# Where four weight sets of an FFN lie in their buffers: 0, 16, 32 and 48 bytes in, not 64

## The chip, the cores and the metric

The kernel runs on one core of one Trainium2 chip. The metric is the device time of one execution in microseconds (us), lower is better; the time before is the median of three runs.

## The reference

One layer of a streaming encoder over 512 positions and 1,024 channels, all in float32: an RMS norm, one wide input projection, three mixers (pooling, a gated linear recurrence, stick-breaking attention), a gated sum of their projections, an output projection with residual, and behind that an FFN. The change lies in the FFN, which is

```python
h2 = rms_norm(x, norm_ffn[l])
act = jax.nn.silu(jnp.einsum('bsd,df->bsf', h2, w_ffn_gate[l])) * jnp.einsum('bsd,df->bsf', h2, w_ffn_up[l])
x = x + jnp.einsum('bsf,fd->bsd', act, w_ffn_down[l])
```

with 2,816 inner columns, and `rms_norm` divides by the root of the mean square over the channels.

## The kernel before

**Products.** TensorE is fed with numbers of reduced width (`F32R`). To keep the accuracy, each operand is split into a high part and a low part (ScalarE copies the high part, VectorE subtracts it from the operand), and each product takes three matmuls: high by high, high by low, low by high. Large products are computed as 2 by 2 blocks with seven block products in place of eight (Strassen's scheme in Winograd's form). The seven are called "11", "12", "S1", "S2", "S3", "S4" and "22". Where this is done, half of the 512 positions go through a matmul at a time, so a matmul there has 256 columns; elsewhere it has 512.

**A weight set.** One of the seven block products of one chunk needs one weight set: 128 partitions by 1,024 elements, as a high and a low tile. It feeds 24 matmuls: 2 column groups, 4 steps along the contraction, 3 matmuls each. Each set is loaded (a `raw`, `wr`, `wa`, `wb` or `wc` tile), perhaps summed with another block, and split into two tiles of the pools `whi` and `wlo`. Each of these pools has three buffers, so a split waits until TensorE is done with the set three places earlier.

**Offsets.** A buffer of these pools has 1,024 + 128 elements, and the set can lie anywhere in the first part of it: `weight_tiles` takes the offset `o` in elements of 4 bytes. Three constants and lists matter: `OFF = 16` (64 bytes) is the usual offset of a set in the seven-product stages; `STEPS = (0, 4, 8, 12)` (0, 16, 32 and 48 bytes) is used up by the first four sets of each such stage; sets of the other stages lie at 0. There are four stages with sets of this kind: the gates (`goffs`), the third branch projection (`boffs`), the FFN's gate and up projection, and the down projection (both `offs`).

In the program's layout a buffer of `whi` or `wlo` starts 96 bytes behind a multiple of 128, and so does each operand tile that streams through the weights in these stages. A set at 64 bytes therefore starts 32 bytes behind a multiple of 128.

**The FFN's loop.** `steps` lists 77 weight sets: pairs of chunks of 256 inner columns, for each pair the seven products in `ORDER7`, each product for both chunks of the pair, and at the end one chunk alone. In the loop over `steps` the sets are split three ahead by `make_a(n + 3)`; `made[0]` counts the sets that were split. `split_a` takes the next offset from `offs`, or `OFF` when it is empty. `product7` issues the 24 matmuls (the line recorded as L1466), L1333 and L1336 are the splits.

**The mean square.** The FFN's norm is applied late: the products run on the unnormalised input, and the factor `rb2` is multiplied into the results. The sum of squares over the channels is a matmul with a matrix of ones, `rms2` (L1436): four matmuls of 256 columns, all with the same weights `onesr`. It is called in front of step 12 (counted from 0), so it stands in TensorE's queue between the sets 12 and 13. Sets 13 and 14 are "S4" of the chunks 0 and 1, sets 15 and 16 "11" of the chunks 2 and 3. `onesr` is a slice that begins `OFF` elements into its own tile; as laid out, this slice starts 96 bytes behind a multiple of 128.

Of the kernel before, what the change touches and what calls it, by code (L numbers as in the profile page):

```python
# [65 lines left out]
def layer_kernel(ctx: ExitStack, tc: tile.TileContext, x, xt, vecs, w_in, w_qkv7, w_gate7, w_pool, w_rg, w_ig,  # L66
# [1186 lines left out]
    with ExitStack() as ffn:  # L1253
# [21 lines left out]
        A = {}  # L1275
        made = [0, 0, 0]
        offs = []

        def fsrc(c, nm):
            return w_ff7[c, CH[nm], KH[nm]]  # L1280
# [8 lines left out]
        def load_to(upto):  # L1289
            while made[1] < min(upto, DOWN):  # L1290
                load_a(made[1])
                made[1] += 1

        def fetch_a(upto):
            while made[2] < min(upto, len(steps)):
                c, nm = steps[made[2]]
                made[2] += 1
                if nm in ("12", "22"):
                    WR[c, nm] = t = wp.tile([P, 2, 4, P], F32, tag="raw", name=f"wr{c}_{nm}")
                    nc.sync.dma_start(t, fsrc(c, nm))  # L1300

        def sum_a(c):
            if c < DOWN and c not in WC:
                WC[c] = (g4 if c < 2 else corner)([2, 4, P], f"wc{c}")
                i = dve.tensor_tensor(WC[c], WB[c], WA[c], ALU.add)
                if c >= 2:
                    tc.keep_in_program_order(i)

        def make_a(upto):
            while made[0] < min(upto, len(steps)):  # L1310
                c, nm = steps[made[0]]
                made[0] += 1
                if made[0] == 1:
                    offs.extend(STEPS)
                load_to(steps[min(made[0] + 11, len(steps) - 1)][0] + 1)
                fetch_a(made[0])
                src = WR.pop((c, nm)) if nm in ("12", "22") else {"1": WB, "2": WC, "4": WC}.get(nm[1:], WA)[c] \
                    if nm[0] == "S" else WA[c]
                A[c, nm] = split_a(src, f"f{c}_{nm}", 5 < made[0] < 10)
                if nm == "11":  # L1320
                    sum_a(c)
                    nc.gpsimd.dma_start(WA[c], fsrc(c, "21"), accum_op=ALU.add)
                if nm == "S2" and c < LAST:
                    nc.gpsimd.dma_start(WC[c], fsrc(c, "12"), accum_op=ALU.add)
                if nm == "12" and c == LAST:
                    dve.tensor_tensor(WC[c], WC[c], src, ALU.add)
                fetch_a(made[0] + 2)

        def split_a(src, n, pin=False):
            o = offs.pop(0) if offs else OFF  # L1330
            h, l = (t.rearrange("p (w k c) -> p w k c", w=2, k=4)
                    for t in weight_tiles("wh" + n, "wl" + n, o))
            i = act(h, src, AF.Copy)  # L1333
            if pin:
                tc.keep_in_program_order(i)
            dve.tensor_tensor(l, src, h.bitcast(F32), ALU.subtract)  # L1336
            return h, l
# [23 lines left out]
        def in_place_t(nm, half):  # L1361
            hold["t", nm] = t = hold["t", "S1"]
            for c in range(2):
                v = t[:, 2 * c:2 * c + 2, :]
                dve.scalar_tensor_tensor(v, v, -1.0, ys[2 + c][:, :, half], ALU.mult, ALU.subtract)
            split_b(nm)
# [7 lines left out]
        for c in range(4):  # L1374
# [10 lines left out]
            if c == 3:  # L1385
                make_a(3)
# [86 lines left out]
        def split_act(kc):  # L1473
            if kc < NF // 2:
# [7 lines left out]
                 "22": ("y", 0, True, None, None), "S4": ("x", 1, False, None, None)}  # L1482
        banks, parts = {}, {}
        after = {2: [lambda: in_place_t("S2", hi)], 5: [third_t], 7: [lambda: in_place_t("22", lo)], 9: [rms2_sum],
                 12: [rms2]}
        for n, (c, nm) in enumerate(steps):
            for f in after.get(n, ()):
                f()
            if (c, nm) == (LAST, "12"):
                split_act(KD)  # L1490
            make_a(n + 3)
            z, half, first_, t_, ts_ = PLAN7[nm]
            if (c, z) not in banks:
                banks[c, z] = fp.tile([P, 2, S], F32, tag="mm", name=f"ps_{z}{c}")
            ps = banks[c, z]
            product7(A.pop((c, nm)), BF[nm], ps, half, first_)
            if t_ is not None:
                if (c, t_) not in parts:
                    parts[c, t_] = g4([2, S], f"t{t_}{c}")
                with tc.high_priority(EARLY):  # L1500
                    act(parts[c, t_][:, :, ts_], ps[:, :, hi], AF.Copy, scale=-1.0 if t_ == "y" else 1.0)
            if bg and n >= 18:
                bg.pop(0)()
            tx, ty = parts[c, "x"], parts.get((c, "y"))
            if nm == "22":
                dve.tensor_tensor(ty, ty, ps, ALU.subtract)
            if nm == "S4":
                dve.tensor_tensor(tx, tx, ps, ALU.add)
            if nm == (LONE if c == LAST else ORDER7)[-1]:
                acts.append(tx)  # L1510
                bg.extend([lambda t=ty: scaled(t), lambda t=tx: scaled(t), lambda x=tx, y=ty: gated_act(x, y)])
            if nm == "S3" and c < LAST:
                sum_a(min(c + 2, LAST))
# [211 lines left out]
```

## Time and profile before

| what | us |
|---|---|
| median of 3 runs | 903.66 (903.24 to 904.38) |
| the profiled execution, whole time | 903.32 |
| the profiled execution, span of the instructions | 901.5 |
| TensorE, matmuls busy | 895.3 |
| VectorE busy | 723.3 |
| ScalarE busy | 531.2 |

PE stands for TensorE's matmuls, PEld for its weight loads, DVE for VectorE, ACT for ScalarE, POOL for GpSimd, SP for SyncE. The matmuls of a stream overlap (one of 256 columns is recorded with some 280 ns), so what one costs in the stream is the distance from its start to the next one's, not its own duration. The chain of waits is the work that ended last, followed back from the end; a row of it gives the start, the length and the number of instructions that follow each other on one line, and its length by that number is the pace.

### The profile page before, as it was taken

How to read it: one execution, taken by the hardware profiler on the slowest of the kernel's cores; microseconds unless marked ns; L12 is line 12 of the kernel's file. 1: busy time of each engine (PE TensorE's matmuls, PEld its weight loads, DVE VectorE, ACT ScalarE, POOL GpSimd, SP SyncE). 2: the span in 40 equal slices, each digit the busy share in tenths (PEclk: the TensorE clock that was granted, in tenths of full speed). 3: DMA queues.
4: the chain of work that ended last, by engine and by line, in shares of the span. 5: the costliest groups of instructions: out<-in, count | busy, mean ns of one | idle time of the engine just before them, and what ended most of it. 6: DMA issues, size and time to landing. Idle time of an engine off the chain costs nothing.

```text
span 901.5 us, 14312 instructions
## 1 busy us (share of the span) xinstructions
PE 895.3 (99%) x5641; PEld 803.8 (89%) x5641; DVE 723.3 (80%) x900; ACT 531.2 (59%) x737; POOL 114.3 (13%) x158
## 2 busy tenths in 40 slices
PE   8999999999999999999999999999999999999998
PEld 6888778888899888888888988999999999989998
DVE  6797887988786599967887694999769596988884
ACT  7554989556856556555664544676555554653542
POOL 2010002232323101000001100111111110101200
PEclk9999999999999999999999999999999999999999
DMA  9495336798682786644635967979677776846842
GB/s 342 130 305 158 117 117 214 219 298 251 179 264 71 232 235 192 217 118 144 214 98 148 196 184 245 260 184 198 157 184 202 172 171 203 202 150 126 196 100 94
DMA packets 85283, 168.77 MB, mean 187 GB/s; under 512 B 8032, under 2 KB 48992, under 8 KB 85216
## 3 DMA queue, kind: packets, MB, share of 16 engines
q1 hardware_dynamic: 68368, 107.24, 35.6%
q0 software_dynamic: 16560, 60.30, 31.0%
q8 instruction: 44, 0.72, 0.3%
q10 hardware_dynamic: 288, 0.32, 0.1%
q14 instruction: 23, 0.19, 0.1%
HBM read 147.39 MB, written 18.87 MB: 184 GB/s over the span
## 4 chain that ended last, share of the span: by engine, by line
PE 94%; DVE 2%; ACT 2%; issue 1%; DMA 0%; ACTq 0%; DVEq 0%
PE ps_y L1466 14%; PE ps_x L1466 10%; PE ps_q L795 7%; PE ps_dy L283 5%; PE ps_dx L283 4%; PE ps_br L274 3%; PE ps_br L275 3%; PE ps_br L276 3%; PE ps_bY L1235 2%; PE ps_gate L698 2%; PE ps_gy L283 2%; PE ps_gate L276 2%; PE ps_bX L1235 2%; PE ps_gx L283 2%; PE ps_gate L275 2%; PE ps_gate L274 2%
## 5 line engine op out<-in xcount | busy, mean ns | idle before, releaser
L109 ACT ACTIVATE whi<-raw 128x1024 fp32r<-128x1024 f32 x65 | 68.8, 1058 | 79.2 <-PE ps_br L275 14.7
L110 DVE TENSOR_TENSOR wlo<-raw,whi 128x1024 fp32r<-128x1024 f32 x65 | 79.3, 1219 | 36.1 <-ACT whi L109 35.9
L110 DVE TENSOR_TENSOR wlo<-qw,whi 128x1024 fp32r<-128x1024 f32 x48 | 58.5, 1221 | 20.8 <-ACT whi L109 20.5
L109 ACT ACTIVATE whi<-qw 128x1024 fp32r<-128x1024 f32 x48 | 50.7, 1057 | 33.1 <-PE ps_q L795 18.6
L1333 ACT ACTIVATE whf_S<-wc 128x1024 fp32r<-128x1024 f32 x22 | 23.3, 1060 | 23.3 <-PE ps_y L1466 12.6
L1336 DVE TENSOR_TENSOR wlf_S<-wc,whf_S 128x1024 fp32r<-128x1024 f32 x22 | 26.9, 1221 | 12.4 <-ACT whf_S L1333 12.3
L1336 DVE TENSOR_TENSOR wlf<-wr,whf 128x1024 fp32r<-128x1024 f32 x22 | 26.8, 1220 | 8.5 <-ACT whf L1333 8.4
L1333 ACT ACTIVATE whf<-wr 128x1024 fp32r<-128x1024 f32 x22 | 23.3, 1060 | 14.9 <-PE ps_y L1466 11.9
L1051 DVE TENSOR_TENSOR_SCAN E<-K,ahead 128x512 f32<-128x512 f32 (+3 forms) x32 | 25.3, 812 | 4.4 <-ACT K L1047 4.4
L1333 ACT ACTIVATE whdS<-dw 128x1024 fp32r<-128x1024 f32 x16 | 17.0, 1064 | 19.1 <-PE ps_dy L283 9.9
L274 PE MATMUL ps_br<-yHH,whi 128*128 128x512 f32 x64 | 25.3, 395 | 0.0
L274 PE MATMUL ps_lru<-HH,whi 128*128 128x512 f32 x64 | 25.2, 394 | 0.0
L274 PE MATMUL ps_br<-yph,whi 128*128 128x512 f32 x64 | 25.2, 394 | 0.0
L274 PE MATMUL ps_pool<-HH,whi 128*128 128x512 f32 x64 | 25.2, 394 | 0.0
L274 PE MATMUL ps_gate<-HH,whi 128*128 128x512 f32 x64 | 25.0, 391 | 0.0
L275 PE MATMUL ps_br<-ypl,whi 128*128 128x512 f32 x64 | 25.0, 391 | 0.0
L276 PE MATMUL ps_br<-yph,wlo 128*128 128x512 f32 x64 | 25.0, 391 | 0.0
L276 PE MATMUL ps_gate<-HH,wlo 128*128 128x512 f32 x64 | 25.0, 391 | 0.0
L275 PE MATMUL ps_br<-yHL,whi 128*128 128x512 f32 x64 | 25.0, 390 | 0.0
L276 PE MATMUL ps_pool<-HH,wlo 128*128 128x512 f32 x64 | 25.0, 390 | 0.0
L276 PE MATMUL ps_br<-yHH,wlo 128*128 128x512 f32 x64 | 25.0, 390 | 0.0
L275 PE MATMUL ps_pool<-HL,whi 128*128 128x512 f32 x64 | 25.0, 390 | 0.0
(706 smaller groups left out, 3558.0 us busy)
## 6 DMA issues: line engine op xcount, KB each, us to landing
raw<-in_w_in_dram SPq DMA_DIRECT2D x31, 512.0 KB, 5.3
qw<-in_w_qkv_dram SPq DMA_DIRECT2D x24, 512.0 KB, 6.7
wr<-in_w_ff_dram SPq DMA_DIRECT2D x22, 512.0 KB, 3.9
raw<-in_w_branch_dram SPq DMA_DIRECT2D x16, 512.0 KB, 3.8
dw<-in_w_down_dram POOLq DMA_DIRECT2D x16, 512.0 KB, 6.3
qw<-in_w_qkv_dram POOLq DMA_DIRECT2D x12, 512.0 KB, 7.9
qd<-r POOLq DMA_DIRECT2D x12, 512.0 KB, 7.3
at<-qd SPq DMA_DIRECT2D x24, 256.0 KB, 5.6
```

Source lines behind the costliest of these rows:

```text
L109: act(hi, raw, AF.Copy)
L110: dve.tensor_tensor(lo, raw, hi.bitcast(F32), ALU.subtract)
L274: nc.tensor.matmul(ps, lh, rh, start=start, stop=False, skip_group_check=skip)
L275: nc.tensor.matmul(ps, lh, rl, start=False, stop=False, skip_group_check=skip)
L276: nc.tensor.matmul(ps, ll, rh, start=False, stop=stop, skip_group_check=skip)
L283: nc.tensor.matmul(o, a_[a][:, w, k, :], b_[b][:, k, :], start=first and n == k == 0, stop=last and n == 2 and k == 3, skip_group_check=True)
L795: nc.tensor.matmul(ps[:, a, :], b_[:, k, ts_], a_[:, kk, :], start=first and n == k == 0, stop=n == 2 and k == 3, skip_group_check=True)
L1051: dve.tensor_tensor_scan(E[:, c0:c0 + n][:, ::-1], K[:, c0 + 1:c0 + n + 1][:, ::-1], ahead[:, S - n:][:, ::-1], 0.0, ALU.mult, ALU.add)
L1235: nc.tensor.matmul(o, ah[x_][:, w, k, :], b[k][y_], start=first_ and n == k == 0, stop=n == 2 and k == 3, skip_group_check=True)
L1333: i = act(h, src, AF.Copy)
L1336: dve.tensor_tensor(l, src, h.bitcast(F32), ALU.subtract)
L1466: m = nc.tensor.matmul(o, a_[x_][:, w, k, :], b_[k][y_], start=first and n == k == 0, stop=n == 2 and k == 3, skip_group_check=True)
```

## The change

The list `STEPS` is put into `offs` a second time, in front of the set with which `made[0]` reaches 13, so that sets 13 to 16 lie 0, 16, 32 and 48 bytes into their buffers; from set 17 on it is 64 again. The step at which `rms2` is called gets a name and stays 12. In the built program no instruction is added, taken away or moved on any of the five queues; the start addresses of the weights of 96 matmuls, and of the 8 splits that write them, are all that differs.

```diff
+        RMS_AT = 12
...
             while made[0] < min(upto, len(steps)):
                 c, nm = steps[made[0]]
                 made[0] += 1
-                if made[0] == 1:
+                if made[0] in (1, RMS_AT + 1):
                     offs.extend(STEPS)
...
         after = {2: [lambda: in_place_t("S2", hi)], 5: [third_t], 7: [lambda: in_place_t("22", lo)], 9: [rms2_sum],
-                 12: [rms2]}
+                 RMS_AT: [rms2]}
```

## The prediction

> **What bounds the kernel now.** I read the page first (busy times, then the chain), then the chain of waits in order of time for the stages whose matmuls are 256 columns wide, and last the single instructions at the seams that it shows.
>
> ```profile
> PE 895.3 (99%) x5641; PEld 803.8 (89%) x5641; DVE 723.3 (80%) x900; ACT 531.2 (59%) x737; POOL 114.3 (13%) x158
> PE 94%; DVE 2%; ACT 2%; issue 1%; DMA 0%; ACTq 0%; DVEq 0%
> PE ps_y L1466 14%; PE ps_x L1466 10%; PE ps_q L795 7%; PE ps_dy L283 5%; PE ps_dx L283 4%; PE ps_br L274 3%; PE ps_br L275 3%; PE ps_br L276 3%; PE ps_bY L1235 2%; PE ps_gate L698 2%; PE ps_gy L283 2%; PE ps_gate L276 2%; PE ps_bX L1235 2%; PE ps_gx L283 2%; PE ps_gate L275 2%; PE ps_gate L274 2%
> ```
>
> TensorE is the bound: the chain that ends last lies on it for 94% of the span, and the FFN's seven-product loop (L1466) alone is 14 + 10 = 24%. So what counts is how fast TensorE takes its matmuls one after the other. A weight set is 24 matmuls of 256 columns. Here is that loop in the chain of waits (start us, us, what, number of matmuls), with rows left out where the same lengths repeat:
>
> ```profile
> 571.43 5.71 PE ps_y L1466 x48
> 577.14 11.11 PE ps_x L1466 x96
> 588.25 16.32 PE ps_y L1466 x144
> 604.57 0.48 PE ps_rms L1436 x4
> 605.04 5.65 PE ps_x L1466 x48
> 610.70 5.65 PE ps_y L1466 x48
> 616.35 11.31 PE ps_x L1466 x96
> 627.66 16.96 PE ps_y L1466 x144
> ...
> 746.38 16.96 PE ps_y L1466 x144
> ```
>
> The same instruction at the same shape has two paces. Sets 7 to 12 take 16.32 us for 144 matmuls: 113.3 ns each, 2.72 us a set. Then come the four matmuls of the mean square, and from there on the same 144 take 16.96 us: 117.8 ns each, 2.827 us a set, unchanged from 605 to the loop's end. Nothing waits at that seam, and the granted clock (the column of 1.00) is full on both sides of it:
>
> ```profile
> core 0: us, PE busy (x) PEld busy (x) DVE busy (x) ACT busy (x) POOL busy (x), PEclk, DMA share, GB/s
> 588.00:604.00 16.00, 16.00 (x144) 16.00 (x143) 14.66 (x14) 11.76 (x15) 1.69 (x2) 1.00 0.83 201
> 605.00:625.00 20.00, 20.00 (x172) 20.00 (x171) 19.77 (x22) 13.74 (x19) 2.53 (x3) 1.00 0.81 176
> 705.00:745.00 40.00, 40.00 (x342) 40.00 (x341) 30.87 (x29) 21.05 (x26) 4.22 (x5) 1.00 0.69 173
> ```
>
> So the slow pace is neither the clock nor a late operand: it is a state of TensorE's own stream, and it lasts once entered. The other three stages with 256-wide matmuls show how it is left. Gates, branch, and down projection, from the same view:
>
> ```profile
> 260.99 2.87 PE ps_gy L283 x24
> 263.86 2.84 PE ps_gx L283 x24
> 266.71 2.84 PE ps_gy L283 x24
> 269.55 2.83 PE ps_gx L283 x24
> 272.37 2.72 PE ps_gy L283 x24
> ...
> 489.03 2.87 PE ps_bY L1235 x24
> 491.90 5.68 PE ps_bX L1235 x48
> 497.58 2.83 PE ps_bY L1235 x24
> 500.41 2.72 PE ps_bX L1235 x24
> ...
> 821.45 11.38 PE ps_dy L283 x96
> 832.83 21.76 PE ps_dx L283 x192
> ```
>
> In each, four sets run at 2.87, 2.84, 2.84 and 2.83 us, and from the fifth on every set takes 2.72. Those four are the sets which lie 0, 16, 32 and 48 bytes into their buffers, and the fifth is the first at 64. The FFN does it too (5.71 for sets 1 and 2; 11.11 less two sets of 2.72 leaves 5.67 for 3 and 4). Four of four climbs end in the fast pace.
>
> **The change, part by part.** The program's instructions, their order on each queue and their number stay as they are; only the start addresses of 96 matmuls' weights (and of the splits by ScalarE and VectorE that write them) move, in sets 13 to 16.
>
> *Sets 13 to 16.* Now they take 5.65 + 5.65 = 11.30 us. If they repeat the climb, they take what the down projection's row shows for its four: 11.38. Cost: 0.08 us, all on the path.
>
> *Sets 17 to 77.* These are 61 sets at 64 bytes, now at 16.96/6 = 2.827 us. At the fast pace each takes 16.32/6 = 2.72. Gain: 61 x 0.1067 = 6.51 us, all on the path.
>
> *Why I take the fast pace.* What must be like the four known cases is the state from which the climb starts. The first set of a stage, at 0 bytes, falls into a beat of 120 ns; the mean square's matmuls do the same before set 13 begins. Weight loads of set 1, and then of the seam:
>
> ```profile
> 571.50 0.19 PEld L1466 LDWEIGHTS ps_y<-h2h,whf 128*128 128x128 f32 x1
> 571.62 0.19 PEld L1466 LDWEIGHTS ps_y<-h2l,whf 128*128 128x128 f32 x1
> 571.74 0.19 PEld L1466 LDWEIGHTS ps_y<-h2h,wlf 128*128 128x128 f32 x1
> ...
> 604.29 0.54 PEld L1436 LDWEIGHTS ps_rms<-sqr,onesr 128*128 128x128 f32 x4
> 604.76 0.19 PEld L1466 LDWEIGHTS ps_x<-h2h,whf_S 128*128 128x128 f32 x1
> ```
>
> In set 1 the loads start 0.12 us apart. At the seam, four loads of the ones fill 604.29 to 604.76, some 118 ns each, and their matmuls 604.57 to 605.04 (0.48 us, 120 ns each). The addresses agree: as the program lays them out, the slice of ones starts 96 bytes behind a multiple of 128, as a set at 0 bytes does, while a set at 64 bytes starts 32 behind one. So today the stream goes from the ones straight to sets at 64 bytes, the jump that no stage start makes, and stays slow. After the change set 13 has the phase of the ones, and the rest is the climb of the other stages. One difference remains: they come from 512-wide matmuls, this one from four 256-wide ones. For the fast pace without it there is only the price of today, 2.827; with it, 2.72. I take 2.72, by four rows against one difference.
>
> *Splits.* ACT and DVE write the same 1,024 elements to other addresses; sets 1 to 4 already have these offsets. Taken as 0; were a split 0.1 us longer, it would vanish in the slack below.
>
> *What hides behind the faster pace.* TensorE must find its weights ready. The splits wait for TensorE to give buffers back (three per kind), not for loads:
>
> ```profile
> ACT whf_S L1333 <- PE ps_x L1466: 24.8, 17, 1.8
> ACT whf_S L1333 <- PE ps_y L1466: 19.7, 14, 1.8
> ACT whf L1333 <- PE ps_y L1466: 19.3, 17, 1.8
> ```
>
> (who waited for whom between 560 and 790; us, times, longest). No split in that list waits for a DMA. Splits tied to the release move along with TensorE. The one tight place is set 19, where VectorE, busy 19.77 of 20 us with the inverse root and the first scalings, is late:
>
> ```profile
> 620.15 2.35 DVE L1336 TENSOR_TENSOR wlf<-wr,whf 128x1024 fp32r<-128x1024 f32 x2
> ...
> 621.96 0.19 PEld L1466 LDWEIGHTS ps_x<-h2h,wlf 128*128 128x128 f32 x1
> ```
>
> The first of those two subtractions (620.15 and half of 2.35: about 621.4) is needed at 621.96: 0.6 us to spare. After the change TensorE is there 0.08 later for the climb and 2 x 0.107 earlier for sets 17 and 18: 621.83, about 0.45 to spare. VectorE's work before it hangs on sets 13 and 14, which move by under 0.1. Without that cover, the cost is the missing tenths of a microsecond, and a possible fall out of the fast pace (a rival). Beyond 625, VectorE is busy 30.87 of 40; the same work in 38.5 us is 80%, which still fits.
>
> *Behind the loop.* The down projection starts some 6.4 us earlier with its loads tied to the same buffers; its 512-wide matmuls and its own climb are not touched. Taken as 0.
>
> *Sum.* +0.08 - 6.51 = -6.43 us. The profiled execution took 903.32 us (901.5 of span and 1.8 around it), which gives 896.9; the median of the three runs is 903.66, 0.34 above, so I say **897.2**.
>
> **Rivals.**
>
> *No effect: the climb doesn't work from here.* The address of a weight would matter nothing, or the four cases turned fast through what went before (512-wide matmuls), not through the offsets. Sets 17 to 77 stay at 2.827 and sets 13 to 16 cost 0 to 0.08: 903.7. For it speaks that the start differs, and that in the branch stage one set at 64 bytes right behind 512-wide matmuls and a wait came out at nearly the fast pace without any climb:
>
> ```profile
> 526.48 0.23 PE ps_out L275
> 526.71 2.76 PE ps_bY L1235 x24
> ```
>
> So the climb isn't the only way in. Against it: the four climbs switch at the same set, though what ran before differs (gates behind query products, FFN behind the output projection). The Trainium skill, "TensorE: Matmul & The Clock Gate", in the steps of "What happens when you issue a matmul", says that TensorE has two independent read ports into SBUF, so that loading the next weights takes nothing from the running matmul; by that, the weights' address would cost nothing and the time would stay at 903.7. The trace doesn't agree that nothing else sets the pace: 120, 117.8 and 113.3 ns stand for one shape at one clock. Chance 0.09.
>
> *Slower: the climb ends in the worse beat.* The offsets move the stream out of today's 117.8 ns and leave it at the 120 ns of set 1 (2.87 to 2.88 us a set). The price is 61 x (2.88 - 2.827) = 3.2 us, with 0.1 for the climb: 907.0. It decides at set 17: its loads would start 0.12 apart. For it: 120 ns is a beat that holds for a whole set; against it: in no row does a set at 64 bytes keep it. Chance 0.03.
>
> *Fast, then lost.* The climb works, TensorE waits for set 19, and falls back to 117.8 ns. Then the gain is 2 x 0.107 less 0.08: 903.5. For it: the thin 0.45 us; against it: the wait at 526 above ended in the fast pace, not out of it. Were it lost somewhere else, evenly over the loop, half the gain is left: 900.4. Chance 0.04 for both.
>
> **How the numbers follow.** The climb works: 0.84, and the time is 897.2. The measured medians of a kernel differ by some tenths (903.24 to 904.38 in three runs), so its own range is 896.2 to 898.4. That is more than 0.8 already, so the range needn't reach to the rivals at 903.5 and above; for a stall of a tenth at set 19 I put 0.1 at either end: 896.1 to 898.5. 0.2% is 1.8 us, about what a measurement of this kernel can tell from no change. Faster: 0.84 and the half of the lost cases that are lost midway, 0.86; same: no effect and the other half, 0.11; slower: 0.03.
>
> **What would show it.** In the chain of waits after 604.57, two rows of 48 that add up to about 11.38; then rows of 96 at 10.88 and of 144 at 16.32 in place of 11.31 and 16.96, up to a loop end at about 782.3 in place of 788.8. Weight loads of set 17 would start 0.113 apart. Down projection: again 11.38, then 21.76 for 192. No idle time of TensorE at 621.8. The forecast is wrong if set 17 keeps 2.83 (no effect) or 2.88 (slower), or if rows of 144 turn from 16.32 to 16.96 midway (lost).

## The result and the profile after

The changed kernel takes 897.05 us (median of 4 runs, 896.80 to 898.33) against 903.79 for the kernel before (4 runs): a ratio of 0.9928, 95% interval 0.9911 to 0.9945. The profiled execution took 896.80 us, of which 895.0 are its span. In the chain of waits (start us, us, what, number of matmuls; the code stands one line lower, so the loop is L1467 now):

```profile
571.14 5.71 PE ps_y L1467 x48
576.85 11.16 PE ps_x L1467 x96
588.01 16.45 PE ps_y L1467 x144
604.46 0.48 PE ps_rms L1437 x4
604.94 5.72 PE ps_x L1467 x48
610.66 5.67 PE ps_y L1467 x48
616.33 10.88 PE ps_x L1467 x96
627.21 16.32 PE ps_y L1467 x144
...
741.45 16.32 PE ps_y L1467 x144
...
814.91 11.38 PE ps_dy L283 x96
826.29 21.76 PE ps_dx L283 x192
```

Up to the mean square the loop is as before, but for two short waits (11.16 in place of 11.11, 16.45 in place of 16.32). Sets 13 to 16 take 5.72 + 5.67 = 11.39 us. From set 17 on, 96 matmuls take 10.88 and 144 take 16.32, up to the loop's end at 782.25 (779.53 and the 2.72 of the last set), where it was 788.78. The down projection is unchanged. The weight loads at the end of set 16 and the start of set 17 (the load of 616.05 is the first of set 17) show the turn itself:

```profile
615.93 0.19 PEld L1467 LDWEIGHTS ps_y<-h2h,wlf 128*128 128x128 f32 x1
616.05 0.19 PEld L1467 LDWEIGHTS ps_x<-BS1h,whf_S 128*128 128x128 f32 x1
616.17 0.19 PEld L1467 LDWEIGHTS ps_x<-BS1l,whf_S 128*128 128x128 f32 x1
616.28 0.19 PEld L1467 LDWEIGHTS ps_x<-BS1h,wlf_S 128*128 128x128 f32 x1
616.39 0.19 PEld L1467 LDWEIGHTS ps_x<-BS1h,whf_S 128*128 128x128 f32 x1
```

They start 0.12 us apart up to 616.17, and 0.11 to 0.12 (113.3 ns on the mean of the rest of set 17) from there on: one matmul into set 17 the stream is in the fast beat.

### The profile page after: what moved, and what is told of

Read it like the earlier page. It is cut to its first block, busy times and chain, and to the rows that moved or that the text cites. A ratio compares the mean times of both kernels' runs of the same rounds, so it can differ in the third digit from the quotient of the medians.

```text
span 895.0 us, 14312 instructions
## 1 busy us (share of the span) xinstructions
PE 889.6 (99%) x5641; PEld 797.7 (89%) x5641; DVE 723.4 (81%) x900; ACT 531.7 (59%) x737; POOL 113.5 (13%) x158
## 4 chain that ended last, share of the span: by engine, by line
PE 94%; DVE 2%; ACT 2%; issue 1%; DMA 0%; ACTq 0%; DVEq 0%
PE ps_y L1467 13%; PE ps_x L1467 10%; PE ps_q L795 7%; PE ps_dy L283 5%; PE ps_dx L283 4%; PE ps_br L274 3%; PE ps_br L275 3%; PE ps_br L276 3%; PE ps_gate L698 2%; PE ps_bY L1235 2%; PE ps_gy L283 2%; PE ps_gate L276 2%; PE ps_bX L1235 2%; PE ps_gx L283 2%; PE ps_gate L275 2%; PE ps_gate L274 2%
## 5 line engine op out<-in xcount | busy, mean ns | idle before, releaser
L1337 DVE TENSOR_TENSOR wldS<-dw,whdS 128x1024 fp32r<-128x1024 f32 x16 | 19.6, 1223 | 7.0 <-ACT whdS L1334 6.8
```

## The experiments

Below, an address is given modulo 128 bytes as the program lays it out: 96 for a set at 0 bytes; 112, 0 and 16 for the other three sets of the climb; 32 for a set at 64 bytes. The operand that streams through the weights starts at 96 in all of these stages. Each kernel is compared with runs of the kernel before on the same chip.

**e1_ones: the ones at the sets' own address.** The kernel before, and no second climb.

```diff
-        onesr = cst.tile([P, P + OFF], F32R, tag="onesr", name="onesr")[:, OFF:]
+        onesr = cst.tile([P, P + OFF], F32R, tag="onesr", name="onesr")[:, 0:P]
```

> The kernel before, with the slice of ones at the start of its tile: it then starts 32 bytes behind a multiple of 128, like a weight set at 64 bytes, not 96 behind one. Nothing else changes. Theory (the start address of the weights, modulo 128, moves TensorE's stream into or out of its fast beat; the mean square's matmuls threw it out because their ones lay at another address): the four matmuls of the mean square take 4 x 113 ns = 0.45 us in the chain and sets 13 to 77 stay at 2.72 us. Gain against the kernel before 65 x 0.107 = 6.9 us: about 896.6, some 0.5 below the changed kernel. Rival (any four foreign matmuls throw it out, or the other operand or another accumulator does): 2.83 us from set 13 on, 903.7.

Measured: 897.17 us against 904.53 (0.9918, 0.9902 to 0.9935). The chain of waits at the seam:

```profile
605.77 0.45 PE ps_rms L1436 x4
606.22 5.44 PE ps_x L1466 x48
611.66 5.44 PE ps_y L1466 x48
617.10 11.02 PE ps_x L1466 x96
628.12 16.32 PE ps_y L1466 x144
```

The mean square's matmuls run at 113 ns, and sets 13 and on stay fast (the 11.02 holds a wait of about 0.14 at set 19). So neither four foreign matmuls nor their other operand or accumulator threw the stream out: the address of the ones did.

**e2_jump: set 13 at 0 bytes, then 64 at once.** In the changed kernel the second `STEPS` is `(0,)`.

> Set 13 lies at 0 bytes as in the changed kernel, but set 14 and all behind it at 64 at once. Theory (the climb by 16 bytes per set carries the stream over; a jump by 64 does not, as the jump from the ones to 64 bytes in the kernel before did not): set 13 at 2.88 us, then 2.83 for the rest, 903.8. Rival (any change of address behind the mean square will do, or a whole set at 0 bytes is what counts): 2.72 from set 14 on, about 896.7.

Measured: 903.57 us (one run). In its chain, 605.24 to 610.94 holds sets 13 and 14 (5.71: 120.0 and 117.8 ns from load to load), and then come

```profile
610.94 5.65 PE ps_y L1467 x48
616.59 11.31 PE ps_x L1467 x96
627.90 16.96 PE ps_y L1467 x144
```

The slow beat lasts to the loop's end. One set at 0 bytes is not what helps.

**e4_half: steps of 32 bytes.** The second `STEPS` is `(8,)`: from the ones at address 96 to set 13 at address 0 and set 14 at address 32, two steps of 32 bytes.

> The climb behind the mean square has one step: set 13 lies at 32 bytes, set 14 and all behind it at 64. The ones act as the set at 0, so the steps are 32 and 32 bytes. Theory in its strict form (steps of 16 bytes are needed): 2.83 us from set 14 on, 903.7. Theory in its loose form (each step must only be shorter than 64 bytes): one set of about 2.84, then 2.72, gain 64 x 0.107 = 6.8 us, about 896.9. Rival (the address does not matter): 903.7.

Measured: 903.53 us (one run).

```profile
605.24 5.67 PE ps_x L1467 x48
610.90 5.65 PE ps_y L1467 x48
616.56 11.31 PE ps_x L1467 x96
627.86 16.96 PE ps_y L1467 x144
```

Set 13 takes 118.2 ns a matmul, and all behind it 117.8, as in e2_jump. So of the steps tried so far, those of 64 and 32 bytes miss the fast beat and those of 16 reach it, where nothing waits in between: the strict form holds.

**e3_late: the second climb at sets 33 to 36.** `if made[0] in (1, 33)`.

> The second climb is made by sets 33 to 36, in the middle of the slow stretch, not by 13 to 16. Theory (a set at 0 bytes brings the stream to its 120 ns beat whatever beat it had, so a climb can start anywhere): 2.83 us up to set 32, a set of about 2.88, three of about 2.84, and 2.72 from set 37 on; gain 41 x 0.107 - 0.1 = 4.3 us, about 899.4. Rival (the climb works only behind matmuls that already run at the 120 ns beat, as the ones do): 2.83 to the end, 903.7.

Measured: 900.86 us (one run), 1.5 above what the theory said. Its chain has two parts:

```profile
589.44 16.96 PE ps_y L1467 x144
606.40 0.47 PE ps_rms L1437 x4
...
652.10 5.65 PE ps_y L1467 x48
657.75 11.38 PE ps_x L1467 x96
669.13 16.55 PE ps_y L1467 x144
685.68 5.44 PE ps_x L1467 x48
```

The late climb did what was expected. The 5.65 holds sets 29 and 30, the 11.38 sets 31 to 34 and the 16.55 sets 35 to 40; from load to load, sets 31 and 32 run at 117.8 ns, 33 at 120.0, 34 and 35 at 118.4, 36 at 117.8, and from set 37 on all run at 113.3. So a climb starts as well from the 117.8 ns beat. What was not expected stands in the first row: sets 7 to 12 were slow, though the first climb had been made. Its weight loads show why; TensorE waited between sets 4 and 5 for ScalarE's copy out of an accumulator (the first row below is the last load of set 4):

```profile
582.93 0.19 PEld L1467 LDWEIGHTS ps_x<-BS1h,wlf_S 128*128 128x128 f32 x1
583.52 0.19 PEld L1467 LDWEIGHTS ps_x<-h2h,whf 128*128 128x128 f32 x1 [0.40 <-ACT ty L1502]
583.62 0.19 PEld L1467 LDWEIGHTS ps_x<-h2l,whf 128*128 128x128 f32 x1
583.75 0.19 PEld L1467 LDWEIGHTS ps_x<-h2h,wlf 128*128 128x128 f32 x1
```

Behind the wait the stream came back in the 117.8 ns beat and stayed there: 8 sets x 0.107 = 0.9 us, and 0.5 for the wait, are most of the 1.5. Up to set 12 this is the changed kernel's own program, and there the same wait ended fast. So the changed kernel's gain has a soft spot, which the next runs looked at.

**e7_noclimb: e1_ones without a climb in the FFN's loop.** The `offs.extend(STEPS)` of `make_a` is taken out.

> The ones as in e1_ones, and no climb in the FFN's loop: all its 77 sets lie at 64 bytes from the first on; the other three stages keep theirs. Theory (the jump by 64 bytes from the 512-wide matmuls, whose weights lie at 0, leaves the stream in the slow beat, as the jump from the ones did; nothing behind it brings it over, but a wait may): 2.83 us for all sets unless TensorE waits, so about 77 x 2.827 against e1's 4 x 2.845 + 73 x 2.72: 7.7 us over e1_ones, about 904.5. Rival (a set at 64 bytes is fast whatever came before, and only the ones disturbed it): 2.72 for all sets, 0.5 us below e1_ones, 896.4.

Measured: 897.79 us (one run), between the two theories, and the chain says why:

```profile
572.37 5.66 PE ps_y L1464 x48
578.02 11.36 PE ps_x L1464 x96
589.38 16.45 PE ps_y L1464 x144
605.84 0.45 PE ps_rms L1434 x4
606.29 5.44 PE ps_x L1464 x48
```

The jump from 512-wide matmuls does end in the slow beat (5.66 for sets 1 and 2; the weight loads of sets 1 to 4 are 117.8 ns apart). Then TensorE waited for the same copy, here 0.37 us from load to load, and came back fast, some six matmuls behind the wait. So the rival is wrong that a set at 64 bytes is fast by itself, and a wait can also bring the fast beat.

**e8_on: climb on to 128 bytes.** From e1_ones; sets 13, 14, 15 at 80, 96 and 112 bytes, all behind them at 128, which is address 96 again.

> The ones as in e1_ones; behind the mean square the sets climb on by 16 bytes each: set 13 at 80 bytes, 14 at 96, 15 at 112, and 16 to 77 at 128, where the weights start 96 behind a multiple of 128 like a set at 0. It tells whether the fast beat belongs to the address or to the way there. Theory A (address and beat belong together: at 0 modulo 128 the beat is 120 ns): from about set 16 on 2.88 us, 62 x 0.16 = 9.9 us over e1_ones, about 906.5. Theory B (the climb shifts the stream once, and then any fixed address keeps it): 2.72 throughout, 896.7. Between: the 117.8 ns beat, 903.5.

Measured: 906.69 us (one run).

```profile
605.05 5.67 PE ps_x L1470 x48
610.72 5.76 PE ps_y L1470 x48
616.48 11.52 PE ps_x L1470 x96
628.00 17.28 PE ps_y L1470 x144
```

17.28/144 = 120 ns: theory A, which said 906.5. At address 96 the beat is 120 ns, however gently one arrives. So the fast beat needs both an address and a way there: at 96 there is one beat (120), at 32 there are two (113.3 and 117.8), and the way, or a wait, decides between them. A single step of 16 bytes off address 32 ended the fast beat: from load to load, set 13 at address 48 took 118.7 ns, 14 at 64 took 117.4 and 15 at 80 took 119.9. Of the eight addresses 16 bytes apart at which a whole set lay in these kernels, 32 alone showed 113.3; six of the others were held for one set only.

**e6_twosets and e5_fine: a shorter climb in all four stages.** Both have the ones of e1_ones. The pieces of a set lie apart, so that the set itself climbs: in e6 its two halves are 16 bytes off each other (`STEPS = ((0, 4, 2), (8, 4, 2))`, a first offset, a gap, a number of pieces, in elements), in e5 its eight blocks 8 bytes (`STEPS = ((0, 2, 8),)`).

> Like e5_fine, but the climb takes two sets, in four steps of 16 bytes with 12 matmuls at each. Theory: two sets at 2.83 to 2.88 us, fast from the third on, 8 x 0.11 = 0.9 us below e1_ones, about 896.0. Rival (24 matmuls are needed at each step): slow from the third set on, 905 to 911.

> The ones start 32 behind a multiple of 128 as in e1_ones, and the climb at the start of each of the four stages takes one set, not four: the set's eight blocks of 128 columns lie 8 bytes further apart than they need to, so its weights start 0, 8, 16 to 56 bytes in, three matmuls at each, and the second set is at 64 already. Theory (small steps carry the stream over; how many matmuls run at each step doesn't matter): one set of about 2.85 us, then 2.72; three sets less at the slow pace in four stages, 12 x 0.11 = 1.3 us below e1_ones, about 895.5. Rival (the stream needs more than three matmuls to settle at each step): slow from the second set on in all four stages, 13 sets of the gates, 13 of the branch, 76 of the FFN, 27 of the down projection, up to 129 x 0.107 = 13.8 us over e1_ones less some, 905 to 911.

Measured: e6 895.85 us against 903.61 (0.9916, 0.9901 to 0.9930; 895.52 to 896.18 in 4 runs), near the 896.0 of the theory: twelve matmuls at a step are enough. e5 900.5 us (0.9959, 0.9935 to 0.9984), with 10 runs anywhere from 895.19 to 906.38. First the gates of e5, then its FFN:

```profile
261.10 2.83 PE ps_gy L297 x24
263.93 2.72 PE ps_gx L297 x24
266.65 2.72 PE ps_gy L297 x24
...
588.46 16.96 PE ps_y L1479 x144
605.42 0.47 PE ps_rms L1449 x4
605.89 5.46 PE ps_x L1479 x48
611.35 5.44 PE ps_y L1479 x48
616.79 11.18 PE ps_x L1479 x96
627.97 16.96 PE ps_y L1479 x144
```

The climb works with three matmuls at each step of 8 bytes: in all four stages the second set is fast. In this execution the FFN loses the beat afterwards, twice: at a wait at set 8 (231 ns from load to load) and at one at set 19 (210 ns), and between them it is fast again from the mean square's matmuls on. Its wait behind set 4 was the longest of all, 1051 ns, and ended fast. Nothing in e5 behind set 19 would restore the beat. The lowest run, 895.19, is near the theory's 895.5; the median is not, and I had not expected the spread. The highest, 906.38, is more than a beat lost over all the FFN's sets but the first explains (895.19 + 76 x 0.107 = 903.3). That run has no profile, and the rest stays open.

**c_after, c_e6 and e9_again: can it be made to last?** The changed kernel and e6_twosets again, and e6 with one more climb of one set at set 21, behind the usual waits:

```diff
                 if made[0] == 1:
                     offs.extend(STEPS)
+                if made[0] == 21:
+                    offs.extend(((0, 2, 8),))
```

> The changed kernel once more, beside the next two on one chip. Theory: 897.1. Its profile may show waits of TensorE at sets 4 and 8, as the first one did; since the ones bring the stream to the 120 ns beat and the climb follows, a beat lost in sets 5 to 12 costs at most 8 x 0.107 = 0.9 us, so no run should be above 898.5 unless the wait at set 19 loses it for good (58 x 0.107 = 6.2 us, 903).

> e6_twosets once more: the ones at the sets' own address, climbs in two sets. Theory: 895.9 where the beat survives the waits at sets 4, 8 and 19; each run that loses it there ends 6 to 8 us higher (58 to 73 sets x 0.107), since nothing behind brings it back. Rival (waits don't matter to the beat): all runs within 0.5 us.

> e6_twosets with one more climb, in one set (eight steps of 8 bytes, as in e5_fine), at set 21, behind the last of the usual waits. Theory: the climb costs one set at about 2.83 us and 0.1 for the jump down to 0 bytes, 0.1 to 0.2 us, so 896.0 where e6 has 895.9; and no run ends higher than 0.107 x 13 = 1.4 us above that, whatever the waits did. Rival (a climb of one set fails when it starts from the fast beat): 57 x 0.107 = 6 us higher in all runs, 902.

Measured on one chip, against 903.67:

| kernel | median us | runs | ratio, 95% interval |
|---|---|---|---|
| c_after | 897.60 | 6: 897.18 to 898.28, and 900.91 | 0.9937, 0.9924 to 0.9950 |
| c_e6 | 897.13 | 6: 896.06 to 897.38, and 901.98, 902.90 | 0.9941, 0.9919 to 0.9964 |
| e9_again | 895.90 | 4: 895.72 to 896.18 | 0.9911, 0.9898 to 0.9924 |

e9_again has the lowest ratio of all versions: 1.7 us below the changed kernel on the same chip, with the smallest spread of the three, though four runs are few to tell a spread by. Its profiled execution had waits at sets 4, 8 and 19 and kept the beat through all three; set 21 climbed at 118.2 ns a matmul, and set 22 was fast again:

```profile
615.42 11.02 PE ps_x L1481 x96
626.45 16.44 PE ps_y L1481 x144
642.88 5.44 PE ps_x L1481 x48
```

16.44 holds the climb: 0.12 us more than 16.32. So a climb of one set that starts from the fast beat ends in it, and the rival is wrong. That the climb brings a lost beat back is not shown: in this execution there was none to bring back, and e6_twosets, which has no such climb, also ran four times without a loss (895.52 to 896.18). Two of c_e6's six runs lost some 5 and 6 us. That fits the theory's 58 x 0.107 = 6.2 us for a beat lost at set 19, but no profile of them exists; in its profiled run the beat was lost at set 4 and back at the mean square. c_after's 900.91 was not among its expectations (898.5 or 903); no profile of that run exists, so where it lost 3.4 us stays open.

Wait by wait, from the FFN's weight loads in the profiles of all these kernels (start to start, across the wait, 21 in all): behind 154, 168, 211, 226, 226, 233, 235, 236, 239, 240, 240, 240, 257, 350, 366, 415 and 1051 ns the stream was fast; behind 210, 231, 589 and 698 ns it was slow. A wait of 211 ns kept the beat where one of 210 lost it, so its length in whole nanoseconds does not tell the outcome.

## Why the prediction was right, point by point

*TensorE's beat is a state, and the mean square is where it was lost.* Shown: moving the ones alone (e1_ones) removes the loss.

*The climb from the ones is the climb of the stages.* Shown: set 13 runs at 120.0 ns in the changed kernel, 14 and 15 at 118.4, 16 at 117.8, and 17 at 113.3 but for its first loads, the same series as in sets 1 to 5. The difference that I left open, 512-wide matmuls ahead or not, made no difference: e3_late climbs from the middle of the loop as well. That the slow pace "lasts once entered" holds only while nothing interrupts it: in e7_noclimb a wait ended it.

*+0.08 for sets 13 to 16.* Measured 11.39 against 11.30: +0.09.

*-6.51 for sets 17 to 77.* Each takes 2.72 in the profile, as forecast. Over the whole loop the profiled executions differ by (782.25 - 571.14) - (788.78 - 571.43) = -6.24 us. The +0.09 and -6.51 make -6.42; the two short waits at sets 4 and 8, about 0.2 together, which the execution before did not have, are the rest. The loop also began 0.29 earlier for reasons ahead of it. Neither of these two was in the sum, and they nearly cancel; that the whole came out within a tenth of -6.43 (901.5 less 895.0 is 6.5 by the spans) is luck in that part, while the two terms came out as worked out.

*The cover.* Set 19 was a right place to look at, but not the one tight place: the changed kernel's waits came at sets 4 and 8. In the profiled execution its low part is ready at 621.26 and needed at 621.72, 0.46 us, where the forecast said 0.45. In six of the other kernels' profiles TensorE does wait there, by 0.1 us: e1_ones, e5_fine, e6_twosets, e7_noclimb, c_e6 and e9_again.

*The rivals.* "No effect" is out for this change, but it is what a jump (e2_jump) and steps of 32 bytes (e4_half) do. The Trainium skill, in "TensorE: Matmul & The Clock Gate", "What happens when you issue a matmul", says that loading the next weights takes no read bandwidth of SBUF from the running matmul. No run here shows the ports themselves, but what the prediction drew from it, that an address costs nothing, does not hold for this stream: in one loop at a granted clock of 1.0 the runs show 113.3, 117.8 or 120 ns by address and history. "Slower" is what e8_on does, by other addresses and near the forecast price: 120 ns, 906.69 us. "Fast, then lost" was argued down with the one wait that had ended well, at 526 in the branch stage. That was too little: the runs show waits ending either way. The changed kernel's first four runs lie between 896.80 and 898.33; one of the six later ones stood at 900.91. That its two profiled executions came fast out of every wait is luck too, as far as these runs tell: e3_late, with the same program up to set 12, did not.

## What to carry to other kernels

Where a tight stream of like matmuls runs at two paces with no wait and at full clock, measure the start-to-start distance of the weight loads and look at the start addresses of weights modulo 128 bytes, the odd ones out above all: one constant matrix at another address cost about 7 us here (904.53 against 897.17). Then prefer what keeps the stream in its beat (the same address for all, e1_ones). A way back behind the places where a wait may throw it out is cheap (one set, 0.12 us, e9_again), but of the climbs only the one over four sets was seen to bring back a lost beat in mid-loop (e3_late). A beat held by history shows as spread between runs: look at single runs, not at the median alone.

## What the runs showed of the hardware that was not expected

Two stable paces for the same instruction at the same address, 113.3 and 117.8 ns, and a third, 120.0, at another. What it is in TensorE that keeps the beat was not tried, nor whether the weights' address counts by itself or against the streamed operand's, which was at 96 in every kernel.

In e5_fine and c_e6 the mean square's four matmuls, all with the same weights and at the sets' own address, brought the stream from 117.8 back to 113.3 ns, eight matmuls behind their first. Two cases of two; no run was made to test it.

A wait of TensorE can end in either beat, whichever it began in: from slow to fast (e7_noclimb, 366 ns), from fast to slow (e5_fine, 231 and 210 ns).
